# Two MLP fronts of a hybrid encoder kernel: the first weight pair's two blocks side by side, the right factors queued later, and the squares of the residual added on VectorE

## The chip, the cores and the metric

The kernel runs on one core of one Trainium2 chip. The metric is the device time of one execution in microseconds, the median of several runs; smaller is better.

## What is computed

The reference is a trunk of two layers on 512 tokens of width 1024. Cut to what matters here:

```
h = h + mixer(rmsnorm(h, norm_mix[i]))          # layer 0: gated DeltaNet, layer 1: HGRN2
h = h + square(relu(rmsnorm(h, norm_mlp[i]) @ w_up)) @ w_down     # 1024 -> 4096 -> 1024
...
return rmsnorm(h, norm_final)
```

The output must match in float32; each float32 operand is therefore split into a high part in the matmul's own format and a low part (the rest), and each product is three matmuls: high by high, high by low, low by high.

## The kernel before, in words

All activations are held transposed, as 8 blocks (`c` = 0 to 7) of 128 features by 512 tokens: `h[c]` is the residual, `y[c] = (yh, yl)` the split of `h[c]` times the norm's weights. The norm's factor by token is applied later, to the hidden layer's squares, so that the projections need not wait for the sum of squares.

A weight *pair* is 256 output columns of a weight matrix. `weights` loads it by one DMA on the SyncE queue (`raw`) and splits it in two halves: ScalarE casts the high part (L115), VectorE subtracts (L116). `project` runs over the 8 blocks `k` of its input and issues three matmuls for each output block (L127 high weights by `yh`, L128 high by `yl`, L129 low by `yh`). `stream` takes the first `wide` pairs together, so that for each `k` all their output blocks get their three matmuls before the next `k`; the other pairs are done one output block at a time.

The change touches two places in each layer and one between the layers:

- `out_proj` multiplies the mixer's output by its output weights: four blocks side by side (the first two pairs), then blocks 4, 5, 6 and 7 one after the other. For each block, VectorE adds the PSUM result to `h[c]` (L867; in layer 1 it first multiplies by a row factor, L864, and adds in L865), and `renew` makes `yh` (L221) and `yl` (L222) on VectorE, squares `h[c]` on ScalarE (L162, L165) and adds the square to the accumulator `sqacc` (L167).
- `mlp` follows at once. `up_plain(0)` to `up_plain(3)` are the first four pairs of `w_up`, done with plain products (the text calls them pairs 0 to 3): ScalarE takes relu (L893) and square (L880), and the result is split (cast L854, rest L855). Between pairs 0 and 1 the program asks for `rstd_rows`: ScalarE casts `sqacc` (L193), VectorE makes the low part (L194), TensorE sums over partitions with a matrix of ones (L197, two matmuls), and VectorE and ScalarE make the token factor. After pair 1 the program asks for `quarters`, the *right factors*: sums and differences of quarters of `y`, 32 instructions of 256 columns on VectorE (L954, L957, L958, L960, L962 and half of L855) and 20 on ScalarE. They are used by `seven` (the rest of `w_up` by seven products in place of eight), which comes after pair 3 and the first half of a `w_down` group.
- At the end of layer 0's MLP the last columns of `w_down` are done block by block, with `renew` after each (L927); the next mixer follows.

The instruction order on each engine is made by a list scheduler before the run. Each engine then works its own list in order and waits by semaphores. "The front" below is the stretch from `out_proj`'s last blocks to the end of pair 3; there is one in each layer.

Of the kernel before, what the change touches and what calls it, by code (L numbers as in the profile page):

```python
# [11 lines left out]
F32 = mybir.dt.float32  # L12
# [3 lines left out]
ALU = mybir.AluOpType  # L16
# [3 lines left out]
NB = D // P  # L20
# [13 lines left out]
class Net:  # L34
# [824 lines left out]
    def out_proj(self, src, norm, rb=None):  # L859
        nc = self.nc  # L860
        for c, out in enumerate(self.stream(src, self.o, wide=2)):
                if rb is not None:
                    t = self.work("gate", bufs=2)
                    nc.vector.tensor_tensor(out=t, in0=out, in1=rb, op=ALU.mult)  # L864
                    nc.vector.tensor_tensor(out=self.h[c], in0=self.h[c], in1=t, op=ALU.add)  # L865
                else:
                    nc.vector.tensor_tensor(out=self.h[c], in0=self.h[c], in1=out, op=ALU.add)  # L867
                self.renew(c, norm, "v" if c >= NB - 2 else "g")


    def mlp(self, up, down, end, norm, last=False):


        nc = self.nc
        ng = HID // 512
        hid = [[] for _ in range(ng)]

        def hidden(g, z):

            nc.scalar.activation(out=z, in_=z, func=AF.Square)  # L880
            if g >= ng - 2:
                nc.vector.tensor_tensor(out=z, in0=z, in1=self.r2b, op=ALU.mult)
            if g % 2 == 0:
                t = self.work("kq", [P, 2, T], F32R, bufs=4)
                hh, hl = t[:, 0], t[:, 1]
            else:
                hh, hl = (self.work("ol", dt=F32R, bufs=NH) for _ in (0, 1))
            hid[g].append(self.split(z, hh, hl))

        def up_plain(p):  # L890
            for out in self.stream(up[p:p + 1], self.y):
                z = self.work("z", bufs=3)
                nc.scalar.activation(out=z, in_=out, func=AF.Relu)  # L893
                hidden(p // 2, z)

        def up_seven(p):
            for z in self.seven(up[p], quarters):
                hidden(p // 2, z)

        def down_half(g, i):  # L900
            for b, out in enumerate(self.stream(down[2 * g + i:2 * g + i + 1], hid[g])):
                h = self.h[4 * i + b]
                nc.vector.tensor_tensor(out=h, in0=h, in1=out, op=ALU.add)
                if g == ng - 3:
                    nc.vector.tensor_tensor(out=h, in0=h, in1=self.r2b, op=ALU.mult)

        up_plain(0)
        self.r2b, x = self.rstd_rows(square=True)
        up_plain(1)
        quarters = self.quarters(self.nw[:, (norm - 1) * NB:norm * NB])  # L910
        up_plain(2)
        up_plain(3)
        for c in range(NB):
            nc.vector.tensor_tensor(out=self.h[c], in0=self.h[c], in1=x, op=ALU.mult)
        self.two = True
        for g in range(ng - 2):
            for i in (0, 1):
                down_half(g, i)
                up_seven(2 * g + 4 + i)
        self.nw_tiles, self.two = 0, False  # L920
        y = hid[ng - 2] + hid[ng - 1]
        if last:
            for n in (0, 1):
                self.finish(end, y, n)
        else:
            for c, out in enumerate(self.stream(end, y, wide=1)):
                nc.vector.tensor_tensor(out=self.h[c], in0=self.h[c], in1=out, op=ALU.add)  # L927
                self.renew(c, norm, "v" if c >= NB - 2 else "g")

    def quarters(self, w):  # L930


        nc, mul, sub, add = self.nc, ALU.mult, ALU.subtract, ALU.add
        n = T // 2
        t1, t2 = slice(0, n), slice(n, T)
        old = lambda c, t: tuple(p[:, t] for p in self.y[c])
        b = {i: [old(c + d, t) for c in range(4)] for i, d, t in ((1, 0, t1), (2, 4, t1), (3, 4, t2))}
        stt = nc.vector.scalar_tensor_tensor
        for i in (4, 5, 6, 7):
            if i == 4:  # L940
                b[i] = [self.work("v", [P, 2, n], F32R, bufs=4) for _ in range(4)]
            elif i == 7:
                pair = [self.work("uw", [P, 2, 2, n], F32R, bufs=2) for _ in (0, 1)]
                b[i] = [pair[c // 2][:, c % 2] for c in range(4)]
            else:
                b[i] = [self.work("oh", [P, 2, n], F32R, bufs=NH) for _ in range(4)]
            b[i] = [(t[:, 0], t[:, 1]) for t in b[i]]
        for c in range(4):
            h, g = self.h[c], self.h[c + 4]
            w1, w2 = w[:, c:c + 1], w[:, c + 4:c + 5]  # L950
            x, e, s = self.work("x", [P, 2, n]), self.work("e", [P, 2, n]), self.work("gate", [P, n], bufs=2)
            diff, y22, s2, s3, s4 = x[:, 0], x[:, 1], e[:, 0], e[:, 1], s
            nc.scalar.activation(out=y22, in_=g[:, t2], func=AF.Copy, scale=w2)
            nc.vector.tensor_tensor(out=diff, in0=h[:, t2], in1=h[:, t1], op=sub)  # L954
            hi, lo = b[5][c]
            nc.scalar.activation(out=hi, in_=diff, func=AF.Copy, scale=w1)
            stt(out=lo, in0=diff, scalar=w1, in1=hi.bitcast(F32), op0=mul, op1=sub)  # L957
            stt(out=s2, in0=diff, scalar=w1, in1=y22, op0=mul, op1=sub)  # L958
            self.split(s2, *b[6][c])
            stt(out=s3, in0=h[:, t2], scalar=w1, in1=y22, op0=mul, op1=sub)  # L960
            self.split(s3, *b[7][c])
            stt(out=s4, in0=g[:, t1], scalar=w2, in1=s2, op0=mul, op1=add)  # L962
            self.split(s4, *b[4][c])
        return b
# [182 lines left out]
```

## Time and profile before

| | us |
|---|---|
| time, median of 3 runs | 1344.73 |
| lowest and highest run | 1344.09, 1346.52 |
| the profiled execution's own time | 1347.91 |
| its span (first to last instruction) | 1345.3 |

In the profiled execution TensorE's matmuls are busy for 1313.0 us (98%), VectorE 1000.1 (74%), ScalarE 650.8 (48%), GpSimd 100.0 (7%). An engine's list in order of time gives for each instruction its start, its duration, the engine, the line, the operation with output and inputs, and in brackets the time the engine sat idle before it and what ended that. The start of the next instruction often comes before the end of the last, since an engine overlaps the tail of one with the head of the next; "start to start" below means the distance of two starts.

### The profile page before, as it was taken

What the parts mean: (1) busy time and instruction counts of PE and PEld (TensorE: products, weight loads), DVE (VectorE), ACT (ScalarE), POOL (GpSimd) and SP (SyncE); (2) the same over time, 40 slices, a digit from 0 to 9 for tenths busy, and PEclk for the clock granted to TensorE, in tenths of its full rate; (3) what the DMA queues carried; (4) which work ended last, traced back from release to release, by engine and by line L of the source; (5) the groups of instructions that cost most, each with busy time, mean ns of one, the idle gap of its engine ahead of it and who ended that gap; (6) DMA issues with size and microseconds to landing.
All of it is one profiled execution on the core that took longest, in us unless ns stands there. A gap on an engine that the chain in (4) does not pass through costs nothing.

```text
span 1345.3 us, 26503 instructions
## 1 busy us (share of the span) xinstructions
PE 1313.0 (98%) x11204; PEld 1128.9 (84%) x11204; DVE 1000.1 (74%) x1824; ACT 650.8 (48%) x1216; POOL 100.0 (7%) x124
## 2 busy tenths in 40 slices
PE   7999999999989999999999999999999999999997
PEld 4777777877868899898988898898878989999897
DVE  5896777765995787778854897787697767777863
ACT  5663656454464453444523654545354444444452
POOL 4001020200200000000020001000100000000012
PEclk8999999999999999999999999999999999999998
DMA  6130111221312232322231312112132223232252
GB/s 202 36 122 34 65 64 33 80 80 65 119 70 95 94 103 99 113 95 94 95 125 35 124 51 78 64 64 95 63 125 94 95 95 98 98 119 94 95 172 79
DMA packets 23365, 121.69 MB, mean 90 GB/s; under 512 B 3664, under 2 KB 6864, under 8 KB 9680
## 3 DMA queue, kind: packets, MB, share of 16 engines
q1 hardware_dynamic: 23248, 120.02, 26.2%
q8 instruction: 87, 1.43, 0.4%
q14 instruction: 30, 0.25, 0.1%
HBM read 117.91 MB, written 2.10 MB: 89 GB/s over the span
## 4 chain that ended last, share of the span: by engine, by line
PE 85%; DVE 9%; ACT 3%; issue 2%; DMA 0%; POOL 0%; SPq 0%; POOLq 0%; DVEq 0%; ACTq 0%
PE pj L128 18%; PE pj L127 18%; PE pj L129 18%; PE pj L1005 6%; PE pj L1004 6%; PE pj L1003 6%; DVE wlo L116 2%; PE pga L478 1%; PE gr L790 1%; DVE yl L222 1%; DVE yh L221 1%; PE pj L718 1%; PE pj L719 1%; PE pj L717 1%; DVE whi L746 1%
## 5 line engine op out<-in xcount | busy, mean ns | idle before, releaser
L115 ACT CAST whi<-raw 128x1024 fp32r<-128x1024 f32 (+2 forms) x174 | 170.4, 1016 | 198.5 <-PE pj L128 175.7
L127 PE MATMUL pj<-yh,whi 128*128 128x512 f32 x576 | 231.9, 403 | 4.3 <-DVE yh L221 2.6
L128 PE MATMUL pj<-yl,whi 128*128 128x512 f32 x576 | 232.0, 403 | 1.4 <-DVE yl L222 1.4
L129 PE MATMUL pj<-yh,wlo 128*128 128x512 f32 x576 | 230.9, 402 | 0.6 <-POOL wlo L116 0.6
L116 DVE TENSOR_TENSOR wlo<-raw,whi 128x1024 fp32r<-128x1024 f32 (+2 forms) x169 | 201.3, 1209 | 16.6 <-ACT whi L115 16.4
L128 PE MATMUL pj<-ol,whi 128*128 128x512 f32 (+1 forms) x368 | 136.9, 372 | 0.0
L127 PEld LDWEIGHTS pj<-yh,whi 128*128 128x128 f32 x576 | 109.6, 190 | 27.7 <-ACT whi L115 3.6
L128 PEld LDWEIGHTS pj<-yl,whi 128*128 128x128 f32 x576 | 109.4, 190 | 23.0 <-DVE yl L222 2.2
L129 PEld LDWEIGHTS pj<-yh,wlo 128*128 128x128 f32 x576 | 109.2, 190 | 22.5 <-POOL wlo L116 1.1
L129 PE MATMUL pj<-kq,wlo 128*128 128x512 f32 (+1 forms) x320 | 117.6, 369 | 0.5 <-DVE wlo L116 0.5
L127 PE MATMUL pj<-kq,whi 128*128 128x512 f32 (+1 forms) x320 | 118.0, 369 | 0.0
L128 PE MATMUL pj<-kq,whi 128*128 128x512 f32 (+1 forms) x320 | 117.8, 368 | 0.0
L127 PE MATMUL pj<-ol,whi 128*128 128x512 f32 (+1 forms) x304 | 111.4, 367 | 0.0
L129 PE MATMUL pj<-ol,wlo 128*128 128x512 f32 (+1 forms) x304 | 111.3, 367 | 0.0
L128 PEld LDWEIGHTS pj<-ol,whi 128*128 128x128 f32 x368 | 69.5, 189 | 11.2
L129 PEld LDWEIGHTS pj<-kq,wlo 128*128 128x128 f32 x320 | 60.3, 189 | 11.0 <-DVE wlo L116 0.9
L127 PEld LDWEIGHTS pj<-kq,whi 128*128 128x128 f32 x320 | 60.4, 189 | 9.7
L128 PEld LDWEIGHTS pj<-kq,whi 128*128 128x128 f32 x320 | 60.4, 189 | 9.6
L129 PEld LDWEIGHTS pj<-ol,wlo 128*128 128x128 f32 x304 | 57.3, 189 | 9.5
L127 PEld LDWEIGHTS pj<-ol,whi 128*128 128x128 f32 x304 | 57.2, 189 | 9.0
L854 ACT CAST wlo<-raw 128x1024 fp32r<-128x1024 f32 (+1 forms) x48 | 39.7, 826 | 45.8 <-DVE raw L971 41.6
L167 POOL TENSOR_TENSOR sqacc<-sqacc,z 128x512 f32<-128x512 f32 x25 | 37.5, 1501 | 274.8 <-ACT z L165 270.7
(433 smaller groups left out, 3086.6 us busy)
## 6 DMA issues: line engine op xcount, KB each, us to landing
raw<-up SPq DMA_DIRECT2D x32, 1024.0 KB, 4.9
raw<-down SPq DMA_DIRECT2D x24, 1024.0 KB, 4.9
raw<-gdn_in SPq DMA_DIRECT2D x14, 1024.0 KB, 4.8
raw<-end SPq DMA_DIRECT2D x12, 1024.0 KB, 4.9
raw<-hgrn_fq SPq DMA_DIRECT2D x8, 1024.0 KB, 4.9
raw<-gdn_out SPq DMA_DIRECT2D x4, 1024.0 KB, 5.3
raw<-hgrn_i SPq DMA_DIRECT2D x4, 1024.0 KB, 4.9
raw<-hgrn_gate SPq DMA_DIRECT2D x4, 1024.0 KB, 4.9
```

The source lines that it names most:

```text
L115: self.nc.scalar.copy(out=hi[:, k], in_=raw[:, k])
L116: eng.tensor_tensor(out=lo[:, k], in0=raw[:, k], in1=hi[:, k].bitcast(F32), op=ALU.subtract)
L127: mm(o, lhsT=hi[:, k, c], rhs=yh, start=(k == 0), stop=False)
L128: mm(o, lhsT=hi[:, k, c], rhs=yl, start=False, stop=False)
L129: mm(o, lhsT=lo[:, k, c], rhs=yh, start=False, stop=(k == last))
L167: e.tensor_tensor(out=self.sq, in0=self.sq, in1=t, op=ALU.add)
L221: nc.vector.tensor_scalar(out=yh, in0=self.h[c], scalar1=wcol, scalar2=None, op0=ALU.mult)
L222: nc.vector.scalar_tensor_tensor(out=yl, in0=self.h[c], scalar=wcol, in1=yh.bitcast(F32), op0=ALU.mult, op1=ALU.subtract)
L854: self.nc.scalar.copy(out=hi, in_=src)
L1003: mm(out, lhsT=hi[:, k], rhs=yh, start=(k == 0), stop=False)
L1004: mm(out, lhsT=hi[:, k], rhs=yl, start=False, stop=False)
L1005: mm(out, lhsT=lo[:, k], rhs=yh, start=False, stop=(k == 3))
```

## The change

Three edits, the same in both layers:

1. Pair 0 of `w_up` is taken `wide`, so that its two output blocks run side by side: for each `k` six matmuls in place of three, and then the next `k`.
2. `quarters` gets as a second argument the VectorE instruction that ends pair 0's last split. Two of its VectorE instructions for each `c` (L957 and L963 of the changed file) are put behind it in VectorE's order (an order only, without a semaphore), and with them what hangs on them.
3. All squares of `renew` in `out_proj` and in the end of layer 0's MLP are added on VectorE (L167); before, GpSimd added those of blocks 1 to 5.

```
-                self.renew(c, norm, "v" if c >= NB - 2 else "g")        # out_proj, and the end of mlp
+                self.renew(c, norm, "v")
...
-            hid[g].append(self.split(z, hh, hl))
+            nc.scalar.copy(out=hh, in_=z)
+            hid[g].append((hh, hl))
+            return nc.vector.tensor_tensor(out=hl, in0=z, in1=hh.bitcast(F32), op=ALU.subtract)
...
         def up_plain(p):
-            for out in self.stream(up[p:p + 1], self.y):
+            for out in self.stream(up[p:p + 1], self.y, wide=1 - min(p, 1)):
                 z = self.work("z", bufs=3)
                 nc.scalar.activation(out=z, in_=out, func=AF.Relu)
-                hidden(p // 2, z)
+                step = hidden(p // 2, z)
+            return step
...
-        up_plain(0)
+        late = up_plain(0)
...
-        quarters = self.quarters(self.nw[:, (norm - 1) * NB:norm * NB])
+        quarters = self.quarters(self.nw[:, (norm - 1) * NB:norm * NB], late)
...
-            nc.vector.tensor_tensor(out=diff, in0=h[:, t2], in1=h[:, t1], op=sub)
+            self.after(nc.vector.tensor_tensor(out=diff, in0=h[:, t2], in1=h[:, t1], op=sub), late)
...
-            stt(out=s3, in0=h[:, t2], scalar=w1, in1=y22, op0=mul, op1=sub)
+            self.after(stt(out=s3, in0=h[:, t2], scalar=w1, in1=y22, op0=mul, op1=sub), late)
```

In the changed file the lines behind `hidden` stand 2 or 3 further down (L893 is L895, L954 is L957, L903 is L906), and the split of the hidden layer has lines of its own (cast L888, rest L890).

TensorE's list in layer 0, where pair 0 uses the last two blocks of `y` (`yh_4450` is block 6, `yh_4483` block 7; `pj_4498` is pair 0's first output block). Before:

```order
L127 MATMUL pj_4498<-yh_4450,whi_4491 128x512
L128 MATMUL pj_4498<-yl_4451,whi_4491 128x512
L129 MATMUL pj_4498<-yh_4450,wlo_4492 128x512
L127 MATMUL pj_4498<-yh_4483,whi_4491 128x512
L128 MATMUL pj_4498<-yl_4484,whi_4491 128x512
L129 MATMUL pj_4498<-yh_4483,wlo_4492 128x512
L127 MATMUL pj_4529<-yh_4312,whi_4491 128x512
```

and of the changed kernel (`pj_4499` is pair 0's second block):

```order
L127 MATMUL pj_4498<-yh_4450,whi_4491 128x512
L128 MATMUL pj_4498<-yl_4451,whi_4491 128x512
L129 MATMUL pj_4498<-yh_4450,wlo_4492 128x512
L127 MATMUL pj_4499<-yh_4450,whi_4491 128x512
L128 MATMUL pj_4499<-yl_4451,whi_4491 128x512
L129 MATMUL pj_4499<-yh_4450,wlo_4492 128x512
L127 MATMUL pj_4498<-yh_4483,whi_4491 128x512
L128 MATMUL pj_4498<-yl_4484,whi_4491 128x512
L129 MATMUL pj_4498<-yh_4483,wlo_4492 128x512
L127 MATMUL pj_4499<-yh_4483,whi_4491 128x512
```

The first use of block 7 moves from the 22nd matmul of pair 0 to the 43rd.

VectorE's list in layer 0, from `out_proj`'s block 6 to the addition of block 7 (`yh_4450` and `yl_4451` are made from `h[6]`, which is `kd_4191`; `aa_4193` is `h[7]`). Before:

```order
L221 TENSOR_SCALAR yh_4450<-kd_4191,norms 128x512
L957 SCALAR_TENSOR_TENSOR oh_4650<-x_4660,norms,oh_4650 128x256
L222 SCALAR_TENSOR_TENSOR yl_4451<-kd_4191,norms,yh_4450 128x512
L167 TENSOR_TENSOR sqacc_4316<-sqacc_4316,z_4454 128x512
L855 TENSOR_TENSOR oh_4654<-e_4661,oh_4654 128x256
L855 TENSOR_TENSOR v_4646<-gate_4662,v_4646 128x256
L954 TENSOR_TENSOR x_4676<-aa_4181 128x256
L960 SCALAR_TENSOR_TENSOR e_4677<-aa_4181,norms,x_4676 128x256
L958 SCALAR_TENSOR_TENSOR e_4677<-x_4676,norms 128x256
L957 SCALAR_TENSOR_TENSOR oh_4651<-x_4676,norms,oh_4651 128x256
L855 TENSOR_TENSOR uw_4658<-e_4677,uw_4658 128x256
L867 TENSOR_TENSOR aa_4193<-aa_4193,pj_4457 128x512
```

and of the changed kernel (`wlo_719_4578` and `wlo_4726` are the low parts of pairs 1 and 2):

```order
L867 TENSOR_TENSOR kd_4191<-kd_4191,pj_4424 128x512
L221 TENSOR_SCALAR yh_4450<-kd_4191,norms 128x512
L116 TENSOR_TENSOR wlo_719_4578<-raw_4576,whi_718_4577 128x1024
L222 SCALAR_TENSOR_TENSOR yl_4451<-kd_4191,norms,yh_4450 128x512
L167 TENSOR_TENSOR sqacc_4316<-sqacc_4316,z_4454 128x512
L116 TENSOR_TENSOR wlo_719_4578<-raw_4576,whi_718_4577 128x1024
L867 TENSOR_TENSOR aa_4193<-aa_4193,pj_4457 128x512
L221 TENSOR_SCALAR yh_4483<-aa_4193,norms 128x512
L116 TENSOR_TENSOR wlo_4726<-raw_4724,whi_4725 128x1024
L222 SCALAR_TENSOR_TENSOR yl_4484<-aa_4193,norms,yh_4483 128x512
```

The instructions of 256 columns (right factors) are gone from between the two blocks; splits of weights stand there, one of them now between block 7's `yh` and `yl`.

ScalarE's list of the changed kernel in layer 0 from the relu of pair 0's first block on (`z_4560` is the cast of the sum of squares, L193). Before, L193 stood right behind the relu of pair 0's second block; here is the list of the changed kernel:

```order
L895 ACTIVATE z_4548<-pj_4498 128x512
L115 CAST whi_4797<-raw_4796 128x1024
L880 ACTIVATE z_4548<-z_4548 128x512
L895 ACTIVATE z_4554<-pj_4499 128x512
L888 CAST kq_4551<-z_4548 128x512
L880 ACTIVATE z_4554<-z_4554 128x512
L193 CAST z_4560<-sqacc_4316 128x512
```

L193 now has six instructions of pair 0 and pair 3 ahead of it that can only start when pair 0's first block is done. On TensorE the first L197 stands behind the 16th matmul of pair 1 in layer 0 and behind the 12th in layer 1 (before: behind the 9th in both); the second L197 stands two matmuls further on. SyncE's list of DMAs is the same as before.

## Rows read from the trace of the kernel before

**Rows 1.** The profile's page: the chain of work that ended last, by engine, and the row of the weights' low parts among the costliest groups.

```profile
PE 85%; DVE 9%; ACT 3%; issue 2%; DMA 0%; POOL 0%; SPq 0%; POOLq 0%; DVEq 0%; ACTq 0%
L116 DVE TENSOR_TENSOR wlo<-raw,whi 128x1024 fp32r<-128x1024 f32 (+2 forms) x169 | 201.3, 1209 | 16.6 <-ACT whi L115 16.4
```

**Rows 2.** TensorE's waits of the whole run (who waited for whom: us in total, times, longest).

```profile
PE pj L127 <- DVE yh L221: 2.6, 2, 1.4
```

**Rows 3.** TensorE's list in layer 0's front (start, duration, line, idle before).

```profile
367.07 0.39 PE L129 MATMUL pj<-oh,wlo 128*128 128x512 f32 x1
367.29 0.39 PE L127 MATMUL pj<-yh,whi 128*128 128x512 f32 x1
...
373.65 0.51 PE L127 MATMUL pj<-yh,whi 128*128 128x512 f32 x1 [1.44 <-DVE yh L221]
374.71 0.50 PE L128 MATMUL pj<-yl,whi 128*128 128x512 f32 x1 [0.55 <-DVE yl L222]
...
383.27 0.50 PE L197 MATMUL ps<-z,one 128*128 128x512 f32 x1 [0.34 <-ACT z L193]
...
386.42 0.49 PE L197 MATMUL ps<-z,one 128*128 128x512 f32 x1 [1.48 <-DVE z L194]
386.75 0.39 PE L129 MATMUL pj<-yh,wlo 128*128 128x512 f32 x1
...
416.21 0.39 PE L127 MATMUL pj<-kq,whi 128*128 128x512 f32 x1
```

**Rows 4.** TensorE's list in layer 1's front.

```profile
975.21 0.39 PE L128 MATMUL pj<-kq,whi 128*128 128x512 f32 x1
976.08 0.50 PE L129 MATMUL pj<-kq,wlo 128*128 128x512 f32 x1 [0.48 <-DVE wlo L116]
...
992.73 0.50 PE L127 MATMUL pj<-yh,whi 128*128 128x512 f32 x1 [1.17 <-DVE yh L221]
994.05 0.50 PE L128 MATMUL pj<-yl,whi 128*128 128x512 f32 x1 [0.82 <-DVE yl L222]
...
995.28 0.63 PE L129 MATMUL pj<-yh,wlo 128*128 128x512 f32 x1
995.71 0.63 PE L127 MATMUL pj<-yh,whi 128*128 128x512 f32 x1
...
1034.95 0.39 PE L127 MATMUL pj<-kq,whi 128*128 128x512 f32 x1
```

**Rows 5.** Stretches of the run with each engine's busy time; PEclk is TensorE's granted clock as a share of full speed. The columns behind the stretch's length are TensorE's matmuls, its weight loads, VectorE, ScalarE, GpSimd, PEclk, the DMA engines' share and GB/s. The first stretch lies in `out_proj` of layer 0, while four output blocks run side by side; the second goes from `out_proj`'s first addition to that of block 7; the third is the end of layer 0's MLP; the fourth lies in layer 1's front.

```profile
335.00:345.50 10.50, 10.50 (x48) 8.68 (x47) 8.09 (x18) 4.25 (x7) 0.00 (x0) 1.00 0.30 100
343.69:372.19 28.50, 28.50 (x126) 23.27 (x124) 28.50 (x41) 13.09 (x22) 7.68 (x5) 1.00 0.34 122
678.00:711.00 33.00, 33.00 (x147) 27.35 (x146) 20.21 (x26) 8.11 (x11) 8.80 (x7) 1.00 0.25 90
991.00:1003.00 12.00, 10.01 (x36) 7.58 (x35) 12.00 (x26) 7.35 (x16) 0.00 (x0) 0.86 0.21 72
```

**Rows 6.** VectorE's list in layer 0's front.

```profile
345.97 0.48 DVE L221 TENSOR_SCALAR yh<-aa,norms 128x512 fp32r<-128x512 f32 x1
346.37 0.74 DVE L222 SCALAR_TENSOR_TENSOR yl<-kd,norms,yh 128x512 fp32r<-128x512 f32 x1
...
347.63 0.92 DVE L221 TENSOR_SCALAR yh<-n,norms 128x512 fp32r<-128x512 f32 x1
348.47 1.78 DVE L222 SCALAR_TENSOR_TENSOR yl<-aa,norms,yh 128x512 fp32r<-128x512 f32 x1
350.18 1.51 DVE L221 TENSOR_SCALAR yh<-kd,norms 128x512 fp32r<-128x512 f32 x1
...
355.81 1.51 DVE L221 TENSOR_SCALAR yh<-aa,norms 128x512 fp32r<-128x512 f32 x1
...
360.78 0.41 DVE L954 TENSOR_TENSOR x<-kd 128x256 f32<-128x256 f32 x1
...
361.90 1.78 DVE L222 SCALAR_TENSOR_TENSOR yl<-n,norms,yh 128x512 fp32r<-128x512 f32 x1
...
369.06 0.68 DVE L167 TENSOR_TENSOR sqacc<-sqacc,z 128x512 f32<-128x512 f32 x1
...
371.46 0.47 DVE L957 SCALAR_TENSOR_TENSOR oh<-x,norms,oh 128x256 fp32r<-128x256 f32 x1
371.86 0.41 DVE L855 TENSOR_TENSOR uw<-e,uw 128x256 fp32r<-128x256 f32 x1
372.19 0.67 DVE L867 TENSOR_TENSOR aa<-aa,pj 128x512 f32<-128x512 f32 x1
```

**Rows 7.** GpSimd's list in the same stretch.

```profile
346.39 5.01 POOL L167 TENSOR_TENSOR sqacc<-sqacc,z 128x512 f32<-128x512 f32 x3 [35.59 <-ACT z L165]
355.62 1.42 POOL L167 TENSOR_TENSOR sqacc<-sqacc,z 128x512 f32<-128x512 f32 x1 [4.21 <-ACT z L165]
361.72 1.41 POOL L167 TENSOR_TENSOR sqacc<-sqacc,z 128x512 f32<-128x512 f32 x1 [4.68 <-ACT z L165]
```

**Rows 8.** ScalarE's list in layer 0's front, around the cast of the sum of squares.

```profile
381.17 1.06 ACT L115 CAST whi<-raw 128x1024 fp32r<-128x1024 f32 x1
382.12 0.59 ACT L893 ACTIVATE z<-pj 128x512 f32<-128x512 f32 x1
382.61 0.61 ACT L193 CAST z<-sqacc 128x512 fp32r<-128x512 f32 x1
```

More of the change, by code (lines that the diff above doesn't have):

```diff
@@ L927, in mlp, with quarters @@
                 nc.vector.tensor_tensor(out=self.h[c], in0=self.h[c], in1=out, op=ALU.add)
-                self.renew(c, norm, "v" if c >= NB - 2 else "g")
-    def quarters(self, w):
+                self.renew(c, norm, "v")
+    def quarters(self, w, late):
         nc, mul, sub, add = self.nc, ALU.mult, ALU.subtract, ALU.add
```

## Prediction

> **What bounds the kernel now.** I read the chain of waits first: TensorE holds 85% of it, so time comes out only where TensorE stands still or runs slowly [rows 1]. Next TensorE's waits: two of them are on `yh` (2.6 us), and their lines lie in the stretches that the change touches [rows 2]. Then TensorE's own list in each front.
>
> The undisturbed spacing of two matmuls of 512 columns comes from layer 0: from the 15th matmul of pair 1 at 386.75 to the first `w_down` matmul at 416.21 stand 130 matmuls [rows 3], so 29.46 / 130 = 0.2266 us each. From pair 0's first matmul at 367.29 to 416.21 there are 8 blocks of 24 and two L197, 194 matmuls: 43.96 us if nothing waited, 48.92 in the trace. **Layer 0's front loses 4.96 us.** The gaps are in the list: block 7's `yh` (1.44 idle) and `yl` (0.55), the cast L193 (0.34), the low part L194 (1.48); idle is counted after the modelled end of a matmul, so start to start they are somewhat longer. **Layer 1's front** goes from the second matmul of block 6 at 975.21 to 1034.95, 241 matmuls: 54.61 against 59.74, a loss of 5.13 us: a wait for the weights' low part (0.48), `yh` (1.17), `yl` (0.82), and a stretch at half speed right behind them, where matmuls start 0.43 us apart [rows 4]; the granted clock of that stretch is 0.86 on the mean [rows 5], which mixes the two levels of 2.4 and 1.2 GHz. The two fronts together lose 10.1 us; the end of layer 0's MLP loses nothing (TensorE 33.00 of 33.00 us busy [rows 5]).
>
> Why is block 7's `y` late? Block 7's last matmul starts at 367.07 and takes 0.39 [rows 3], but VectorE gets to its addition only at 372.19: it is 4.7 us behind, and busy for all the 28.50 us from the first block's addition at 343.69 on [rows 5]. Two things put it behind [rows 6, 7]. Five `yh` and `yl` that met a GpSimd addition took 0.92, 1.78, 1.51, 1.51 and 1.78 us where undisturbed ones take 0.48 and 0.74: 0.44 + 1.04 + 1.03 + 1.03 + 1.04 = 4.6 us. And 13 right-factor instructions, the first at 360.78 and the last at 371.86, cost 0.33 to 0.40 start to start (371.46, 371.86, 372.19): 4.3 to 5.2, taken as 4.8.
>
> **Side by side.** Nothing is added: pair 0 has 48 matmuls either way, and its second PSUM block is one that `out_proj`'s block 6 has left. But block 7's `y` is first used by the 43rd matmul, not the 22nd: 42 x 0.2266 = 9.5 us after 367.29, at 376.8, where before it was due at 372.05. Even with `yh` and `yl` as late as now (first uses 373.65 and 374.71) it would be in time. This alone takes the `yh` and `yl` waits.
>
> **The squares.** Five additions leave GpSimd for VectorE at no more than 0.68 us each (the row at 369.06): +3.4 us, and the 4.6 us of hindered `yh` and `yl` go: -1.2. At the end of layer 0's MLP VectorE is busy 20.21 of 33 us [rows 5], so five more additions lie in its gaps and TensorE, which has no wait there, gains and loses nothing.
>
> **The right factors.** 13 instructions go from before block 7's addition: -4.8. In all VectorE would be at block 7's addition at 372.19 - 1.2 - 4.8 = 366.2, before the block is done at 367.46: the backlog is gone. Then addition 0.67, `yh` 0.48; now a half split of pair 2 (1.21, the weights' row [rows 1]) stands between `yh` and `yl` and waits for a ScalarE cast, whose buffer is free when block 7 ends: 367.46 + 1.06 [rows 8] = 368.5, which is no later than `yh`'s end at 368.6. So `yl` ends near 368.6 + 1.21 + 0.74 = 370.6, 6 us ahead of use. Layer 1 has one VectorE instruction more for each block (0.6 to 0.7) and the same shape. Its 0.48 wait for the low part of block 6's weights goes too: in front of that split stood hindered `yh` and `yl`.
>
> Where do the 32 right-factor instructions go? Behind pair 0, some 32 x 0.37 = 12 us of VectorE. Behind them now stand the 8 scalings of `h` (L917 in the changed file), splits of the hidden layer, and the left factors of the first `seven`. Between pair 0's end (367.29 + 48 x 0.2266 = 378.2) and `seven`'s start (194 matmuls and 48 of a `w_down` half after 367.29: 422.1) lie 44 us. The load: 12 for the right factors, 8 x 0.67 = 5.4 for the scalings, 8 hidden splits 5.4, six half splits of weights 7.3, the left factors 7.1 (four additions of 0.67, two splits of 1.21 and three of 0.67, by rows of the same sizes), 2 for the token factor: 39 by full durations, which overlap by about a tenth. It fits, but it is the tightest place of the change. SyncE's list is the same, and the weight buffers are given back no more than some us earlier or later than now; the loads ahead are of pairs that wait.
>
> **What is late next: the sum of squares.** L193 now stands behind pair 0 on ScalarE. Pair 0's first block starts its last matmul four from the end: 367.29 + 44 x 0.2266 = 377.26, done 377.65. ScalarE then does two relus (0.49 start to start), a half cast (0.95: 381.17 to 382.12), two squares and one cast of the same size as L193 (0.5 to 0.6 each): 3.4 to 3.7 us; L193 runs 0.61 and ends at 381.7 to 382.0 [rows 8]. TensorE reaches the first L197 after 48 + 16 matmuls, at 381.8: a wait of 0 to 0.2. L194 on VectorE takes 0.68 more, to 382.4 to 382.7; the second L197 is three positions on, at 382.5 to 382.7. I take 0.25 for both. In layer 1 L193 has no half cast ahead (2.6 to 2.8 us), but L197 stands behind the 12th matmul, 0.9 earlier: 0.3 to 0.4, taken as 0.35. From below it is nothing; from above it is what these two matmuls wait now in layer 0, 0.34 + 1.48 = 1.8, in each front.
>
> **The sum.** Layer 0: -4.96 + 0.25 = -4.7. Layer 1: -5.13 + 0.35 = -4.8, the half-speed stretch included, since it follows the `yh` and `yl` waits that go. Together -9.5: a span of 1345.3 - 9.5 = 1335.8, the profiled execution 1347.91 - 9.5 = 1338.4. That execution is 3.2 above the median of the runs shown, so the forecast of the median is 1344.73 - 9.5 = **1335.2**. Behind each front TensorE is busy without a gap, so what is won at 416 and 1035 is won at the end.
>
> **Rivals.**
>
> *A, the sum of squares takes the wait over (0.15).* If ScalarE or VectorE is late by a us between pair 0 and L197, TensorE waits that us, in both fronts. For it: six instructions that start from pair 0's end stand ahead of L193. Against it: the sum above. Price by the upper bound: 2 x 1.8 less the 0.6 in the sum is +3.0, 1338.2, and up to 1340 if the clock falls to half speed for one stretch as it did in layer 1.
>
> *B, less is lost without the profiler (0.08).* The half-speed stretch stands in one front of two after like waits, so the plain runs may not have it. Seven matmuls at 0.43 for 0.2266 are 1.4 us: 1336.7. With a part of A, 1338 to 1341.
>
> *C, the change does nothing for the time (0.04).* The `y` wait goes, but TensorE runs into the left factors or `w_down` splits that the right factors have pushed back. To eat 9.5 us they must be nearly 5 us late in each front; there are 39 us of full durations for 44. 1342 to 1347.
>
> *D, slower: the clock falls in the side-by-side pairs (0.03).* Pair 0 now changes its PSUM block every three matmuls. If that lets the clock fall to its lower level in both, 48 matmuls at 0.43 cost 48 x 0.2 = 9.8 us in each front: 1335.2 + 19.6 = 1354.8. It decides from 23 matmuls at half speed in each front. Against it: four blocks side by side in `out_proj` run at a granted clock of 1.00 with TensorE busy for 10.50 of 10.50 us [rows 5], and that is the same loop with more blocks. The Trainium skill, TensorE: Matmul & The Clock Gate, section on a second failure mode by depth-cycling of the PSUM queue, tells of a kernel that cycles through PSUM banks and whose clock swings between the levels, because TensorE idles briefly between its groups. By that rule the time would be D's; the row just named disagrees, as there are no idle moments between the groups.
>
> **How the numbers follow.** The forecast has 0.70 (1334 to 1337). 0.2% of the time, 2.7 us, is about what a measurement of this kernel can tell from no change; faster means below 1342.0, which holds for the forecast, A and B: 0.93. Same: C, 0.04. Slower: D, 0.03. The range: nothing below the two fronts' whole loss, 1344.73 - 10.1 = 1334.6, less 1.1 for the runs' scatter (the highest of before is 1.8 above its median, the lowest 0.6 below), 1333.5; above, A with its clock, 1340. It leaves out C, D and a bit of B.
>
> **What would show it.** In the trace after: no wait of TensorE on `yh` or `yl` in the fronts; from pair 0's first matmul to the first `w_down` matmul 44.0 to 44.6 us in both; the granted clock at 1.00 there; all `yh` 0.48 and `yl` 0.74 in both `out_proj`s; VectorE idle before block 7's addition; a wait of some tenths at L197. The prediction is wrong if L197 waits 1 us or more, if TensorE waits before the first `seven`, or if pair 0 shows matmuls 0.43 apart.

## The result, and the profile after

The changed kernel takes 1336.78 us (median of 4 runs, 1335.15 to 1339.58) against 1345.62 for the kernel before in the same session (median of 4): a ratio of 0.9937, 95% interval 0.9917 to 0.9958, so 8.8 us less. The forecast was 1335.2, in a range of 1333.5 to 1340.0.

The waits of the fronts are gone. TensorE's waits of the whole run, after (answers [rows 2]; the longest):

```profile
PE ps L197 <- ACT one L260: 4.4, 1, 4.4
```

It lies at the start of the program; no wait on `yh`, `yl`, L193 or L194 stands in the list any more. TensorE's list after: pair 0's first matmul, the first L197 and the first `w_down` matmul in layer 0 (answers [rows 3]), then the same in layer 1 (answers [rows 4]):

```profile
364.81 0.39 PE L127 MATMUL pj<-yh,whi 128*128 128x512 f32 x1
...
379.42 0.50 PE L197 MATMUL ps<-z,one 128*128 128x512 f32 x1
...
409.06 0.39 PE L127 MATMUL pj<-kq,whi 128*128 128x512 f32 x1
...
978.54 0.39 PE L127 MATMUL pj<-yh,whi 128*128 128x512 f32 x1
...
992.35 0.49 PE L197 MATMUL ps<-z,one 128*128 128x512 f32 x1
...
1022.91 0.39 PE L127 MATMUL pj<-kq,whi 128*128 128x512 f32 x1
```

"Front" below is the time from the first to the third of these rows, 194 matmuls or 43.96 us at the undisturbed spacing. Layer 0: 409.06 - 364.81 = 44.25 us, 48.92 before [rows 3]. Layer 1: 1022.91 - 978.54 = 44.37 us; before it was 1034.95 [rows 4] - 986.64 = 48.31, the start being this row of the list before:

```profile
986.64 0.39 PE L127 MATMUL pj<-yh,whi 128*128 128x512 f32 x1
```

Ahead of layer 1's front the wait for block 6's low part [rows 4] is gone too; start to start it cost 0.87 and 0.34 where 0.23 are usual, 0.75 us. So TensorE won 4.67 us in layer 0 and 3.94 + 0.75 = 4.69 in layer 1, 9.4 in all.

Windows after, columns as in [rows 5]: in layer 0, from `out_proj`'s first addition to block 7's; the end of layer 0's MLP, which now lies seven microseconds earlier than there; and the whole front of layer 1.

```profile
341.21:365.01 23.80, 23.80 (x106) 19.71 (x105) 22.37 (x34) 10.41 (x15) 0.00 (x0) 1.00 0.29 100
671.00:704.00 33.00, 33.00 (x147) 27.32 (x146) 21.09 (x31) 8.11 (x11) 0.99 (x2) 1.00 0.26 89
978.54:1022.91 44.37, 44.32 (x196) 36.26 (x194) 39.61 (x71) 29.02 (x54) 0.00 (x0) 1.00 0.32 112
```

In the first of them VectorE is busy 22.37 of 23.80 us, where it was busy all the time, and GpSimd does nothing. In the second TensorE is busy throughout, as before, with the squares on VectorE. The granted clock is 1.00 in all three. VectorE's list after, from block 7's addition on in layer 0 (answers [rows 6]):

```profile
365.01 0.69 DVE L867 TENSOR_TENSOR aa<-aa,pj 128x512 f32<-128x512 f32 x1 [0.69 <-PE pj L129]
365.73 0.49 DVE L221 TENSOR_SCALAR yh<-aa,norms 128x512 fp32r<-128x512 f32 x1
```

The bracket at L867 is the point: VectorE now waits for TensorE there, where it was 4.7 us late. This holds for layer 0 alone. In layer 1 VectorE stays busy through `out_proj` (24.93 of 25.03 us up to block 7's addition) and comes to that addition without idle time.

The two profiled executions differ by more than the medians (spans 1345.3 and 1333.3, 12.0 us). 2.5 of that (367.29 - 364.81) arise before the first front, in layer 0's mixer, whose code did not change. The largest piece is a stop inside a group of 64 small matmuls; this is TensorE's list before:

```profile
306.26 0.52 PE L523 MATMUL pu<-ud,xd 32*32 32x32 f32 x37 [1.05 <-issue]
```

Such stops are put down to no engine. The longest, near 103 us, stands in every run, while this one is missing in the changed kernel's. They are why the fronts are compared below by their own lengths.

### The profile page after: what moved, and what is told of

Its sections match the earlier page's. It is cut to its first block, busy times and chain, and to the rows that moved or that the text cites. A ratio compares the mean times of both kernels' runs of the same rounds, so it can differ in the third digit from the quotient of the medians.

```text
span 1333.3 us, 26490 instructions
## 1 busy us (share of the span) xinstructions
PE 1310.9 (98%) x11204; PEld 1129.7 (85%) x11204; DVE 997.9 (75%) x1839; ACT 649.5 (49%) x1216; POOL 77.4 (6%) x109
## 4 chain that ended last, share of the span: by engine, by line
PE 87%; DVE 7%; ACT 2%; issue 1%; DMA 1%; SPq 0%; POOL 0%; POOLq 0%; DVEq 0%; ACTq 0%
PE pj L128 19%; PE pj L127 19%; PE pj L129 19%; PE pj L1008 6%; PE pj L1007 6%; PE pj L1006 6%; DVE whi L746 2%; DVE ol L746 1%; PE pga L478 1%; DVE wlo L116 1%; PE pu L523 1%; PE px L516 1%; PE gr L790 1%; PE pw L593 1%; PE pj L718 1%
## 5 line engine op out<-in xcount | busy, mean ns | idle before, releaser
L127 PE MATMUL pj<-yh,whi 128*128 128x512 f32 x576 | 231.9, 403 | 0.8 <-ACT whi L115 0.8
L116 DVE TENSOR_TENSOR wlo<-raw,whi 128x1024 fp32r<-128x1024 f32 (+2 forms) x169 | 200.2, 1203 | 21.3 <-ACT whi L115 21.1
L127 PEld LDWEIGHTS pj<-yh,whi 128*128 128x128 f32 x576 | 109.8, 191 | 22.9 <-ACT whi L115 2.0
L127 PE MATMUL pj<-kq,whi 128*128 128x512 f32 (+1 forms) x320 | 118.0, 369 | 0.0
L127 PE MATMUL pj<-ol,whi 128*128 128x512 f32 (+1 forms) x304 | 111.4, 367 | 0.0
L127 PEld LDWEIGHTS pj<-kq,whi 128*128 128x128 f32 x320 | 60.4, 189 | 9.9 <-issue 0.2
L127 PEld LDWEIGHTS pj<-ol,whi 128*128 128x128 f32 x304 | 57.2, 189 | 9.0
L854 ACT CAST wlo<-raw 128x1024 fp32r<-128x1024 f32 (+1 forms) x48 | 39.7, 827 | 36.9 <-DVE raw L974 34.7
L1008 PE MATMUL pj<-yh,whi 128*128 128x256 f32 x192 | 54.3, 283 | 0.0
```

Source lines behind the costliest of these rows:

```text
L116: eng.tensor_tensor(out=lo[:, k], in0=raw[:, k], in1=hi[:, k].bitcast(F32), op=ALU.subtract)
L127: mm(o, lhsT=hi[:, k, c], rhs=yh, start=(k == 0), stop=False)
L854: self.nc.scalar.copy(out=hi, in_=src)
L1008: mm(out, lhsT=lo[:, k], rhs=yh, start=False, stop=(k == 3))
```

## The experiments

The three edits, alone and left out one at a time, then the suspected cause put back by itself. Each ratio is against runs of the kernel before on the same chip. The theory on record: VectorE's backlog at block 7 (hindered `yh` and `yl`, and right factors ahead) makes `y` late, and each edit takes its share of it. The rival that came up when the instruction lists of the parts were compared: the edits are substitutes, and the list scheduler does part of their work by itself.

| kernel | edits in it | front layer 0 | front layer 1 | ratio to before (95%) |
|---|---|---|---|---|
| before | none | 48.92 | 48.31 | 1 |
| after | all three | 44.25 | 44.37 | 0.9937 (0.9917 to 0.9958) |
| e1_side | side by side | 49.34 | 50.25 | 1.0012 (1.0001 to 1.0022) |
| e2_late | right factors later | 44.15 | 48.58 | 0.9969 (0.9957 to 0.9981) |
| e3_sq | squares | 44.07 | 44.25 | 0.9936 (0.9923 to 0.9949) |
| e4_nosq | side by side, later | 44.26 | 44.26 | 0.9949 (0.9935 to 0.9963) |
| e7_noside | later, squares | 44.16 | 44.31 | 0.9940 (0.9919 to 0.9961) |
| e8_nolate | side by side, squares | 44.21 | 44.19 | 0.9932 (0.9916 to 0.9947) |
| e5_sqtwin | squares, GpSimd kept busy | 45.85 | 45.33 | 1.0003 (0.9991 to 1.0015) |
| e10_aftertwin | all three, GpSimd kept busy | 44.31 | 44.41 | 0.9997 (0.9984 to 1.0010) |
| e6_sqpin | squares, right factors held | 44.44 | 44.29 | 0.9934 (0.9916 to 0.9952) |
| e9_sqpin2 | the same, TensorE's order held | 46.21 | 44.28 | 0.9956 (0.9942 to 0.9970) |

### Side by side alone

```
-            for out in self.stream(up[p:p + 1], self.y):
+            for out in self.stream(up[p:p + 1], self.y, wide=1 - min(p, 1)):
```

> Before with side by side alone; squares on GpSimd and right factors where they were. The theory on record says that this edit alone takes the waits on yh and yl: if nothing else came in, the layer-0 front (pair 0's first matmul to the first w_down matmul, 48.92 us before) would lose 2.2 us less and the layer-1 front (48.31) 3.4 to 3.9 less, the half-speed stretch included, about -5.5 us in all. Rival: VectorE's list is as late as it was, so the same lateness meets TensorE at the next thing that comes from it, the cast of the sum of squares (L193): I expect a wait of about 3 us there in both fronts, fronts of 47.5 to 49 us, and -0.5 to -2.5 us in all. I hold the rival the likelier, since the accumulation of block 7's square stands behind the same backlog.

Measured: 1346.84 us, nothing won, if anything 0.1% lost. TensorE's list, in layer 0 and layer 1:

```profile
383.77 0.79 PE L197 MATMUL ps<-z,one 128*128 128x512 f32 x1 [3.61 <-ACT z L193]
...
1002.21 0.80 PE L197 MATMUL ps<-z,one 128*128 128x512 f32 x1 [3.16 <-ACT z L193]
```

No wait on `yh` or `yl`, as both theories say; but the lateness meets TensorE in pair 1, behind its 16th matmul in layer 0 and its 13th in layer 1, and matmuls behind it start 0.43 us apart. Why is L193 so late? ScalarE's list in layer 0:

```profile
378.64 0.41 ACT L854 CAST oh<-e 128x256 fp32r<-128x256 f32 x1 [0.77 <-DVE e L961]
...
379.63 0.59 ACT L895 ACTIVATE z<-pj 128x512 f32<-128x512 f32 x1
...
383.10 0.61 ACT L193 CAST z<-sqacc 128x512 fp32r<-128x512 f32 x1
```

Ahead of pair 0's relu (L895) stand casts of right factors (L854) that wait for VectorE. The reason given beforehand, the accumulation of block 7's square, is not it: that addition had ended 9.6 us before L193 began.

```profile
372.78 0.67 DVE L167 TENSOR_TENSOR sqacc<-sqacc,z 128x512 f32<-128x512 f32 x1
```

Covering one late product moved the wait to the next one. The rival held in its place, L193, and missed in its size: the fronts are 49.3 and 50.3 us where it named 47.5 to 49, and nothing is won.

### The right factors later, alone

```
-            nc.vector.tensor_tensor(out=diff, in0=h[:, t2], in1=h[:, t1], op=sub)
+            self.after(nc.vector.tensor_tensor(out=diff, in0=h[:, t2], in1=h[:, t1], op=sub), late)
...                                                            # s3 (L963) likewise; nothing else changed
```

> Before with the right factors queued later alone; squares on GpSimd, pair 0 one block after the other. Theory on record: 13 right-factor instructions (4.8 us) go from before block 7's addition, which ends the waits on yh and yl in both fronts alike: about -4.5 in each. Second theory: in layer 1 only three of these instructions stand ahead of block 7's yh before the change, so there the delay is that of the yh and yl which met a GpSimd addition; then layer 0's front falls to 44.0 to 44.5 us, layer 1's stays at 47 to 48.5 with its waits on wlo, yh and yl, and the whole gain is -4 to -6 us.

Measured: 1342.10 us, ratio 0.9969. Layer 0 has its whole gain, layer 1 none. TensorE's list in layer 1:

```profile
986.52 0.49 PE L127 MATMUL pj<-yh,whi 128*128 128x512 f32 x1 [1.42 <-DVE yh L221]
987.79 0.50 PE L128 MATMUL pj<-yl,whi 128*128 128x512 f32 x1 [0.77 <-DVE yl L222]
```

and one of the hindered instructions in VectorE's list there (undisturbed it takes 0.48):

```profile
976.18 1.51 DVE L221 TENSOR_SCALAR yh<-n,norms 128x512 fp32r<-128x512 f32 x1
```

The second theory held: putting the right factors later wins nothing in layer 1. That the three ahead of block 7 cost nothing there is not shown, since with them gone the scheduler put one more split of weights (1.22 us) ahead of block 7's `yh`.

### The squares alone

```
-                self.renew(c, norm, "v" if c >= NB - 2 else "g")
+                self.renew(c, norm, "v")          # both places
```

> Before with the squares on VectorE alone; pair 0 one block after the other and no order forced on the right factors. By the sum on record this is worth 1.2 us of VectorE time in each front, so TensorE would gain about 1.2 us in each, -2.4 in all. Second theory: the list scheduler, with five more additions on VectorE, itself puts most of layer 0's right factors behind block 7 (4 stand ahead of its addition where 13 did), and in layer 1 the hindered yh and yl were the delay; then the waits go in both fronts, both fall to 44.0 to 44.5 us, and this edit alone gives -9 to -9.5 us, as much as all three.

Measured: 1337.31 us, ratio 0.9936: this line alone gives what all three give. From TensorE's list, the ends of both fronts:

```profile
365.33 0.39 PE L127 MATMUL pj<-yh,whi 128*128 128x512 f32 x1
...
409.40 0.39 PE L127 MATMUL pj<-kq,whi 128*128 128x512 f32 x1
...
978.75 0.39 PE L127 MATMUL pj<-yh,whi 128*128 128x512 f32 x1
...
1023.00 0.39 PE L127 MATMUL pj<-kq,whi 128*128 128x512 f32 x1
```

The scheduler had a hand in it, more than I had written beforehand: in layer 0 it puts nine right factors behind block 7's addition, and in layer 1 it lays three of the second block's matmuls in pair 0 ahead of block 7's `yh` product and five more ahead of its `yl` product, a small "side by side" of its own making.

### One part left out at a time

> The changed kernel with the squares of blocks 1 to 5 back on GpSimd; side by side and right factors later are kept. Five yh and yl in each out_proj should be hindered again (0.9 to 1.8 us where 0.48 and 0.74 are usual). If the hindrance matters by itself in spite of the cover that the other two edits give, layer 1's front shows waits on yh, yl or L193 of 1 us and more, and the time is -5 to -7. If the cover is enough, only the 0.5 us wait for the low part of block 6's weights in layer 1 is back: fronts 44.2 to 44.6 us, and -8.5 to -9 us in all.

Measured: 1338.25 us, ratio 0.9949; 0.87 us (start to start) on the low part in layer 1 is back, fronts as with all three. The `yh` and `yl` are hindered again (one `yl` takes 1.78 us), and the other two edits cover it. By the ratio that is 6.9 us less than before, with an interval from 5.0 to 8.7, short of the 8.5 to 9 named for this case; what decides is that the front of layer 1 shows none of the waits that the other case asked for.

> The changed kernel with pair 0's two blocks one after the other again; the right factors later and the squares on VectorE are kept. If VectorE's backlog is gone, side by side has nothing left to cover: fronts 44.0 to 44.3 us as with all three parts, a time within 1 us of the changed kernel's, -8.5 to -9.5. If side by side is still needed as cover, waits on yh or yl of half a microsecond and more stand in layer 1's front, and the time is -6 to -8.

> The changed kernel without the order on the right factors; side by side and the squares on VectorE are kept. The scheduler puts 4 of them ahead of block 7's addition in layer 0 and 2 in layer 1 by itself, as with the squares alone: fronts 44.1 to 44.5 us, a time within 1 us of the changed kernel's, -8.5 to -9.5. By the sum on record, in which the order gives 4.8 us of VectorE time in each front, it would be some 2 to 4 us slower than the changed kernel.

Measured: 1336.92 and 1336.33 us, ratios 0.9940 and 0.9932. Neither loss appears: beside the squares, neither side by side nor the order of the right factors is worth anything that can be measured. (The profiled execution of e7 was 1344.05; its fronts are short, and most of its excess lies ahead of them in layer 0's mixer.)

### GpSimd kept busy

The squares stay on VectorE, but in `out_proj` GpSimd adds the same five squares once more, to `h[c]`, into a tile that nobody reads. The lists of TensorE, VectorE and ScalarE do not change by a row, and the trace names no engine that waits for these additions. (Line numbers stand a little further down: L223 and L224 are `yh` and `yl`, L195 and L199 the cast and the sum of squares.)

```
             e.tensor_tensor(out=self.sq, in0=self.sq, in1=t, op=ALU.add)
+            if twin:                                   # out_proj, blocks 1 to 5
+                nc.gpsimd.tensor_tensor(out=twin, in0=src, in1=t, op=ALU.add)
```

> The squares-alone kernel, and GpSimd does five additions of the same size again in each out_proj, of the same operands into a tile that nobody reads: VectorE's, ScalarE's and TensorE's lists are the same as with the squares alone, only the company on GpSimd is back. If the hindrance of yh and yl by GpSimd is itself what made layer 1's block 7 late, four to five of them take 0.4 to 1.1 us longer; in layer 1 block 7's yh was ready just at its use, so TensorE waits 2.5 to 5 us there; in layer 0 it was ready 3 us ahead, so at most 1.5 us. Time -4 to -6.5 us against the kernel before. If only the order of VectorE's list counted, the fronts stay at 44.1 and 44.3 us and the time at -9.

Measured: 1345.92 us, ratio 1.0003: **the whole gain is gone**. GpSimd's list in layer 0:

```profile
345.28 1.87 POOL L169 TENSOR_TENSOR rB<-aa,z 128x512 f32<-128x512 f32 x1 [35.13 <-ACT z L165]
347.23 1.63 POOL L169 TENSOR_TENSOR rB<-n,z 128x512 f32<-128x512 f32 x1
348.93 1.36 POOL L169 TENSOR_TENSOR rB<-kd,z 128x512 f32<-128x512 f32 x1
354.57 1.87 POOL L169 TENSOR_TENSOR rB<-aa,z 128x512 f32<-128x512 f32 x1 [4.28 <-ACT z L165]
360.73 1.41 POOL L169 TENSOR_TENSOR rB<-n,z 128x512 f32<-128x512 f32 x1 [4.29 <-ACT z L165]
```

VectorE's list beside it:

```profile
346.51 1.19 DVE L224 SCALAR_TENSOR_TENSOR yl<-aa,norms,yh 128x512 fp32r<-128x512 f32 x1
347.62 1.52 DVE L223 TENSOR_SCALAR yh<-n,norms 128x512 fp32r<-128x512 f32 x1
349.06 1.51 DVE L223 TENSOR_SCALAR yh<-kd,norms 128x512 fp32r<-128x512 f32 x1
...
354.62 0.68 DVE L167 TENSOR_TENSOR sqacc<-sqacc,z 128x512 f32<-128x512 f32 x1
355.22 1.76 DVE L224 SCALAR_TENSOR_TENSOR yl<-aa,norms,yh 128x512 fp32r<-128x512 f32 x1
...
360.91 1.51 DVE L223 TENSOR_SCALAR yh<-n,norms 128x512 fp32r<-128x512 f32 x1
```

Every `yh` or `yl` that starts while GpSimd adds ends 0.3 to 0.6 us after GpSimd does. Against 0.48 and 0.74 these five lose 0.45 + 1.04 + 1.03 + 1.02 + 1.03 = 4.6 us. And TensorE's list shows where it is paid, layer 0 and layer 1:

```profile
358.18 0.50 PE L129 MATMUL pj<-oh,wlo 128*128 128x512 f32 x1 [2.27 <-DVE wlo L116]
...
382.92 0.50 PE L199 MATMUL ps<-z,one 128*128 128x512 f32 x1 [1.52 <-ACT z L195]
...
976.28 0.50 PE L129 MATMUL pj<-kq,wlo 128*128 128x512 f32 x1 [2.27 <-DVE wlo L116]
...
981.92 0.50 PE L129 MATMUL pj<-ol,wlo 128*128 128x512 f32 x1 [0.81 <-DVE wlo L116]
...
994.35 0.73 PE L127 MATMUL pj<-yh,whi 128*128 128x512 f32 x2 [0.79 <-DVE yh L223]
```

The three waits on L116 come already in `out_proj`, for the low parts of the weights. Start to start, waits ahead of the front and the front's growth against e3_sq together, layer 1 loses 4.7 us, within the 2.5 to 5 that I expected, but not where: only 0.79 of idle time stands at block 7's `yh`. Layer 0 loses 4.3 where I expected at most 1.5. So the time missed its forecast of -4 to -6.5. I had asked only for block 7's `yh` and not for what the same list owes earlier.

> The changed kernel, with five additions by GpSimd again in each out_proj, into a tile that nobody reads; the lists of VectorE, ScalarE and TensorE are those of the changed kernel to the row. If side by side and the later right factors cover what GpSimd does to yh and yl, the time stays within 2 us of the changed kernel's (-7 to -9 against before). If not, the waits come ahead of the place that they cover, for the weights' low parts in out_proj's blocks 5 and 6, as with the squares alone and the same additions (2.3 us in each layer): I expect that, with -2 to -4 us against before, since the later waits on yh and the sum of squares are covered.

Measured: 1344.77 us, ratio 0.9997. The fronts stay at 44.3 and 44.4 us, so the cover works; but the wait for the low parts ahead of them comes, as expected, and the time is 3 us above the middle of what I expected. In the profiled execution the reason is the clock. TensorE's list in layer 0, and a window of the same stretch:

```profile
360.73 0.61 PE L129 MATMUL pj<-oh,wlo 128*128 128x512 f32 x1 [2.27 <-DVE wlo L116]
361.14 0.63 PE L127 MATMUL pj<-oh,whi 128*128 128x512 f32 x1
```

```profile
360.70:364.50 3.80, 3.77 (x10) 2.96 (x11) 3.80 (x4) 0.63 (x1) 1.22 (x1) 0.55 0.46 110
```

Behind the wait the granted clock is 0.55 on the mean, near the lower of its two levels, and some eight matmuls start 0.43 us apart, in both layers: 2 x 8 x 0.2 = 3.2 us. With the two waits (2.4 and 2.5 us start to start, above the usual spacing) and 0.1 in the fronts that is 8.2 us, and by the medians the loss against the changed kernel is 8.0.

### The right factors held at their old place

Squares alone, and in layer 0 the 13 right factors (a 14th slipped in) are put ahead of block 7's addition in VectorE's order; the weights' split that would follow them there is put behind it.

```
...
+                for p in ((p1, p2, p3, p4, q1, q2, p5, q3) if c == 0 else (p1, p2, p3, p4, q2)):
+                    self.after(self.last_add, p)      # last_add: block 7's addition; layer 0, c = 0 and 1
...
```

> The squares-alone kernel, with the right factors of layer 0 held at their old places: 14 of them ahead of block 7's addition (13 in the kernel before, 4 with the squares alone); layer 1 is as with the squares alone. Theory that the scheduler's own move of the right factors did the work in layer 0: VectorE is again 3.5 to 4 us late at block 7's addition, TensorE waits for yh, yl and the sum of squares, layer 0's front takes 47 to 48.5 us, layer 1's 44.3, and the time is -5 to -7 us. Rival that the end of the hindrance is enough in layer 0 too: front 44 to 45 us, time -8.5 to -9.5.

Measured: 1337.06 us, ratio 0.9934, front 44.44: my theory seemed to fall. But the scheduler had changed TensorE's order as well: four matmuls of pair 0's second block ahead of block 7's `yh` product, four more ahead of the `yl` product. The experiment did not isolate what it should have. Hence once more, with TensorE's order of pair 0 held:

> As e6_sqpin, and TensorE's order of pair 0 in layer 0 is held at that of the kernel before (all 24 matmuls of its first block, then the second block's); in e6_sqpin the scheduler had put four of the second block's matmuls ahead of block 7's yh and four ahead of its yl, which covered a lateness. In e6_sqpin yh was ready 5.73 us after pair 0's first matmul, where 21 matmuls take 4.76: so TensorE should now wait 1.0 us for yh and 0.6 to 0.9 us for yl, layer 0's front should take 45.5 to 46.5 us (44.1 with the squares alone, 48.9 before), and the time is 1.5 to 2.5 us above that of the squares alone, -6 to -7.5 against before. If the 14 right factors ahead of block 7 cost nothing once the hindrance is gone, the front stays at 44 to 44.5.

Measured: 1340.21 us, ratio 0.9956, front 46.21, as expected; the gain of 5.9 us by the ratio is just short of the 6 to 7.5 named, within its interval. TensorE's list in layer 0 (L130 here is the product of L127 in the kernel before, L228 and L229 are `yh` and `yl`):

```profile
366.25 0.39 PE L130 MATMUL pj<-yh,whi 128*128 128x512 f32 x1
...
372.04 0.50 PE L130 MATMUL pj<-yh,whi 128*128 128x512 f32 x1 [0.87 <-DVE yh L228]
373.09 0.50 PE L133 MATMUL pj<-yl,whi 128*128 128x512 f32 x1 [0.56 <-DVE yl L229]
...
412.46 0.39 PE L130 MATMUL pj<-kq,whi 128*128 128x512 f32 x1
```

So the right factors ahead of block 7 cost layer 0's front 2.1 us (46.21 against 44.07) when nothing covers them, and 0.4 when eight matmuls of the other block do. Against the kernel before, this front is 2.7 us shorter, and block 7 has little part in it. The waits on `yh` and `yl` shrank by 0.6 us start to start. Most of the rest is the wait at the two L197, which took 2.4 us in the kernel before. There L194 (at 385.68) stood behind three splits of weights in VectorE's list; in this list the sum of squares comes in time.

## Why the prediction was right, and where it was not

**The total, and the mechanism at block 7.** Forecast -9.5; 9.4 by the two traces' fronts, 8.8 by the medians. What counts is when block 7's `yh` is ready, by VectorE's rows (start and duration), after pair 0's first matmul. Before, in layer 0 and layer 1:

```profile
373.13 0.47 DVE L221 TENSOR_SCALAR yh<-aa,norms 128x512 fp32r<-128x512 f32 x1
...
992.20 0.47 DVE L221 TENSOR_SCALAR yh<-aa,norms 128x512 fp32r<-128x512 f32 x1
```

6.31 us in layer 0 (373.60 - 367.29 [rows 3]) and 6.03 in layer 1, against 21 x 0.2266 = 4.76 where TensorE wants it. After, 1.41 us in layer 0 (365.73 + 0.49 - 364.81); layer 1:

```profile
981.70 0.48 DVE L221 TENSOR_SCALAR yh<-aa,norms 128x512 fp32r<-128x512 f32 x1
```

3.64 us, and wanted only at 9.5. With that the waits on `yh` and `yl` had to go, and the signs named came, but for one: fronts of 44.25 and 44.37 (44.0 to 44.6 were named), clock 1.00, all `yh` and `yl` at their usual length. VectorE is idle ahead of block 7's addition in layer 0 and not in layer 1.

**The step "layer 1 ... has the same shape" is wrong.** The 4.8 us of right factors were counted for both layers. In layer 1's list before, only these three stand ahead of block 7's `yh`, at 992.20:

```profile
984.08 0.41 DVE L954 TENSOR_TENSOR x<-kd 128x256 f32<-128x256 f32 x1
...
990.81 0.47 DVE L957 SCALAR_TENSOR_TENSOR oh<-x,norms,oh 128x256 fp32r<-128x256 f32 x1
...
991.81 0.47 DVE L958 SCALAR_TENSOR_TENSOR e<-x,norms 128x256 f32<-128x256 f32 x1
```

There `yh` came 2.4 us earlier, not 6. e2_late shows it: the order of the right factors gives layer 0 all and layer 1 nothing. The sum survived because it was capped by what TensorE lost, not by what VectorE saved; for layer 1 that was luck.

**The squares, "-1.2", were right at their place and undervalued as an edit.** In e3_sq, layer 1, `yh` is ready 0.8 us earlier than before (983.53 + 0.48 - 978.75 = 5.26):

```profile
983.53 0.48 DVE L221 TENSOR_SCALAR yh<-aa,norms 128x512 fp32r<-128x512 f32 x1
```

Counted from VectorE's first row of `out_proj` (962.27 before, 955.14 here) it is 1.5 earlier: the 1.2, and one right factor fewer. The difference of 0.7 TensorE got ahead of the front, where the wait for block 6's low part is gone. In layer 0, by e9_sqpin2 (right factors still ahead): 371.50 + 0.48 - 366.25 = 5.73, 0.6 earlier. That is 1.2 less one right factor more and a wait of 0.3 in between. The rest of this edit's 8.6 us is for the greater part the scheduler's answer: in layer 0 nine right factors moved (9 x 0.37 = 3.3 us) and L194 no longer late, in layer 1 pair 0's blocks interwoven, and with the waits there the half-speed stretch went (eight matmuls in the trace before, not seven, 1.6 us). I had read the changed kernel's lists only with all three edits in, and put down to the order edit what the squares alone would have brought about.

**"This alone takes the `yh` and `yl` waits"** was right to the word and misleading: alone, side by side moves the wait to the sum of squares, 3.6 and 3.2 us. That is rival A, at twice its price, for the part. For the whole change A did not come: L193 ended 14.55 us after pair 0's first matmul (378.75 + 0.61 - 364.81), TensorE came there at 14.5. Start to start L197 took 0.33 in layer 0 and 0.44 in layer 1 where 0.23 are usual; the fronts lose 0.29 and 0.41 us in all, forecast 0.25 and 0.35. ScalarE's row:

```profile
378.75 0.61 ACT L193 CAST z<-sqacc 128x512 fp32r<-128x512 f32 x1
```

**Two ways to one gain.** Either the squares leave GpSimd, or side by side and later right factors cover the hindrance (e4_nosq). Both together win no more, since little is left to win. The parts' gains add to -1.6 + 4.2 + 8.6 = 11.2 us by their ratios, and the whole is 8.5 by its own: an edit's worth depends on the others present.

**The hindrance** is shown, not only argued: e5_sqtwin and e10_aftertwin change nothing but GpSimd's work and lose all that was won. That e5 loses just what e3 won is chance: VectorE there carries the five additions and the hindrance together, where the kernel before carried the hindrance alone, so the 8.6 us are its price for a VectorE without room and not its share of the loss before. The Trainium skill, SBUF — State Buffer, section Who interferes with whom, says that VectorE and GpSimd share a pair of ports, and that of two instructions that contend for it the first to come has it for its whole length while the other is blocked. The trace agrees: 1.51 for 0.48 and 1.76 for 0.74. The runs show the company and these times; that it is the ports no run here shows. By its row at 354.62, where VectorE's addition of two tiles starts beside GpSimd's, VectorE takes its usual 0.68 and GpSimd 1.87 in place of 1.41.

**Rivals C and D** did not come. The right factors pushed back met nothing: VectorE waits for TensorE again at the first `w_down` addition (0.60 us in both layers). Pair 0's matmuls stand 0.23 apart at a granted clock of 1.00, so alternating between two PSUM blocks does not lower the clock here. Rival B can't be told apart: the median of 1336.78 lies at its price, 1336.7, and 8.8 against 9.4 is within the runs' scatter.

## What to carry to other kernels

Work given to an idle GpSimd is not free when VectorE is the engine that others wait for: here an addition of 0.68 us on VectorE was cheaper than one of 1.4 us on GpSimd that held VectorE's next instruction for 1.0 us. Covering a late product only helps if the next product of the same late engine is not wanted soon; look for it before moving the first. Where a scheduler makes the lists, read the lists of each part alone before splitting a sum among edits, and hold every engine's order when one is to be tested.

## What the runs showed of the hardware that was not expected

The clock after a wait. Behind waits of 3.61 and 3.16 us (e1_side), 2.27 and 2.34 us (e10_aftertwin) and 1.42 with 0.77 us (e2_late) the matmuls start 0.43 us apart for a stretch. Behind the same 2.27 us in e5_sqtwin they don't, in either layer; a window there shows 1.00:

```profile
358.00:366.00 8.00, 7.82 (x34) 6.47 (x35) 8.00 (x11) 2.33 (x3) 1.41 (x1) 1.00 0.45 139
```

The length of one wait alone does not decide it; what does stays open. It makes a wait's price uncertain by some 1.5 to 3 us. In e1_side the stretches behind the two waits cost 1.6 and 2.9 us by TensorE's rows, where the kernel before has one such stretch, of 1.6; with this difference taken off, an estimate from these two traces, side by side alone would have won about a microsecond.
